# A decoder trunk on one core: two more raw weight tiles per group in spare result tiles, the sum t4 made last, the activations transposed two k-tiles later

## The chip, the cores and the metric

The kernel runs on one core of a Trainium2 chip. The metric is the device time of one execution in microseconds (us), the median of several. The core's engines run side by side, each through its own queue of instructions in order: TensorE (PE: matmuls, and PEld for its weight loads), VectorE (DVE), ScalarE (ACT), GpSimd (POOL) and SyncE (SP), which here only issues the DMA transfers from HBM.

## What is computed

256 tokens of width 2048 pass through two layers in float32. Layer 0 mixes by retention, layer 1 by latent attention, and each mixer is followed by a SwiGLU feed-forward of width 5632. The parts that matter here:

```
h = rms_norm(x, norm_mix_pre)
q, k, v, g = split(h @ ret_w_in)              # retention: 8 heads, k 256, v 512
y = retention(rope(q), rope(k), v); h = (silu(g) * groupnorm(y)) @ ret_w_out
x = x + rms_norm(h, norm_mix_post)
h = rms_norm(x, norm_ffn_pre)
gate, up = split(h @ w_gu); x = x + rms_norm((silu(gate) * up) @ w_down, norm_ffn_post)
```

## The kernel before, in words

**Products.** A float32 product is made of three matmuls in a narrower form (fp32r): every operand x is split into hi (x rounded, a cast on ACT, L204) and lo (x minus hi, a subtraction on DVE, L205), and hi·hi, hi·lo and lo·hi are added up in one PSUM bank. The weights arrive as raw tiles of 128 x 1024 float32 (512 KB), are split on the chip, and are the moving operand, 512 columns in one matmul.

**Groups.** A large product is cut into groups. A group multiplies all 256 tokens (two tiles t = 0, 1 of 128) by 1024 columns (two halves c = 0, 1 of 512) over 16 k-tiles, and keeps four PSUM banks (t, c). There are 4 groups for q and k (`qk_group`), 8 for v and g (`vg_group`, one per head) and 11 for gate and up in each layer (`swiglu`). The first group of q/k and of gate/up runs plainly (`group`, L263). All the others run through `first_sevens` (L415).

**first_sevens.** Its first n pairs of k-tiles (n = 4 in gate/up, 3 in v/g, 2 in q/k) are multiplied by a scheme with seven products instead of eight (Strassen's, in Winograd's form), which needs sums of the four blocks b00, b01, b10, b11 of a pair of raw tiles. It comes in stages:

1. `begin(p)`, for each pair p: loads the two raw tiles (L440 into the tag "raw", L443 into "y4"), makes t1 = b00 + b01 (L448), t2 = t1 + b11 (L449) and t3 = b01 + b11 (L452), and splits b00 and t2 (tile b) and t1, t3 (tile a). Nine matmuls of pair p and three of pair p-1 follow. After the last pair, the four banks are combined: m1 is copied out (L471, ACT), u is added up (L475, DVE), v is added in its bank and copied (L478 DVE, L479 ACT), and the banks of c01 (L482) and c11 (L485) are set, both on DVE.
2. `rest(p)`, for each p: splits the second raw tile whole (tile c). Three matmuls per pair go to bank (0,0), then three per pair to bank (0,1), which holds c01.
3. `fourth(p)`, for each p: t4 = t2 + b10 (L463, DVE, in place in t2), split into half a tile d. Three matmuls per pair go to bank (1,0), which must have been copied by L479.
4. The remaining k-tiles (8 in gate/up, kt 8 to 15) run plainly: load, split whole, 12 matmuls each.

**Slots.** Tiles come from tagged pools with a fixed number of slots. "raw" has RAW = 4, the split tiles "whi" and "wlo" have WB = 5 each and "mv" has MV = 6: t2 of every pair, m1 and u lie in "mv". The results of a stage wait in their own tags until its second product: "yT" (8 slots, retention) and "aT" (11 slots, feed-forward). What is not yet filled of these is lent out: `spare` gives the last one or two k-tiles (kt 14 and 15) their hi and lo tiles there. For q/k a tag "spare" of two slots does the same.

**What sets the order.** The source emits a plan; `step()` counts k-tiles, and `later(k, fn)` puts work behind k further ones. The final order on each engine is worked out when the program is built: an instruction whose operands or whose slot are not there yet by that reckoning lets later ones pass. The slots of one tag go out in the order of the source. So DVE, ACT and SP run ahead into the next group while PE works, until slots stop them.

**After a group** of gate/up, ACT makes silu(gate) (L993), DVE the product a (L995, tile "fa"), and `transposes(j, t, a)` (L957) turns it on PE into PSUM (L962, tile "ftp"), from where ACT copies it to aT (L963). `later(2 + t, ...)` on L998 puts these into `begin(1)` of the next group, behind the nine matmuls of pair 0.

**After a group** of v/g, `mixed` (L873) makes the head's output z, which is transposed (L902, "ztp") and copied into yT (L906) at `later(10, ...)`.

Of the kernel before, what the change touches and what calls it, by code (L numbers as in the profile page):

```python
# [8 lines left out]
F32 = mybir.dt.float32  # L9
F32R = mybir.dt.float32r  # L10
# [5 lines left out]
P = 128  # L16
# [41 lines left out]
def trunk(  # L58
# [73 lines left out]
    def later(k, fn):  # L132
        order[0] += 1
        todo.append((steps[0] + k, order[0], fn))
# [63 lines left out]
    wp = ctx.enter_context(tc.tile_pool(name="wp", bufs=1))  # L198
    RAW, WB, MV = 4, 5, 6

    def split(hi, lo, src, g=None):

        if g is None:
            nc.scalar.copy(out=hi, in_=src)  # L204
            nc.vector.tensor_sub(out=lo, in0=src, in1=hi.bitcast(F32))  # L205
        else:
            nc.scalar.activation(out=hi, in_=src, func=AF.Copy, scale=g)
            nc.vector.scalar_tensor_tensor(
                out=lo, in0=src, scalar=g, in1=hi.bitcast(F32), op0=ALU.mult, op1=ALU.subtract
            )  # L210

    def weights(load, parts, name, room=None):

        raw = wp.tile([P, 1024], F32, tag="raw", bufs=RAW, name=f"{name}_raw")
        load(raw)
        if room is None:
            hi = wp.tile([P, 1024], F32R, tag="whi", bufs=WB, name=f"{name}_hi")
            lo = wp.tile([P, 1024], F32R, tag="wlo", bufs=WB, name=f"{name}_lo")
        else:
            hi, lo = room(f"{name}_xhi"), room(f"{name}_xlo")  # L220
        for a, n, g in parts:
            split(hi[:, a : a + n], lo[:, a : a + n], raw[:, a : a + n], g)
        return hi, lo, raw
# [191 lines left out]
    def first_sevens(lhs, kts, w, g, name, n, left, spare):  # L415
# [44 lines left out]
        def fourth(p):  # L460
            if p % 2 == 0:
                last[0] = parts("d")
            nc.vector.tensor_add(out=t2[p], in0=t2[p], in1=raw1[p][:, 0:512])  # L463
            wt["d", p] = half(last[0], p % 2)
            split(*wt["d", p], t2[p])

        kept = {}

# [61 lines left out]
        carry_out(plan, banks, cols, {})  # L530
        return banks

    def tile_load(w, g, name, halves=0, spare=(0, None)):

        def load(kt, first_half=False):
            n = 512 if kt < halves or first_half else 1024

            def dma(raw):
                for a in range(0, 1024, 512 if kt < halves else 1024):
                    m = 512 if kt < halves else 1024
                    nc.sync.dma_start(out=raw[:, a : a + m], in_=w[g, kt, :, a : a + m])

            parts = [(a, n, None) for a in range(0, 512 if first_half else 1024, n)]
            return weights(dma, parts, f"{name}_w{kt}", spare[1] if kt >= DT - spare[0] else None)

        return load

# [186 lines left out]
    def retention():  # L737
# [40 lines left out]
        def vg_group(h, spare):  # L778
            return first_sevens(h_lhs, DT, ret_vg, h, f"rvg{h}", VG_SEVENS, lambda p: ins[p], spare)

        with tc.tile_pool(name="rt_s", bufs=1) as sp:
# [63 lines left out]
            with tc.tile_pool(name="rt_q", bufs=1) as rp:  # L845
                rope_c = rp.tile([P, NT, NF_R], F32, name="rope_c")
                rope_s = rp.tile([P, NT, NF_R], F32, name="rope_s")
                spare = 1, lambda name: rp.tile([P, 1024], F32R, tag="spare", bufs=2, name=name)
                for gq in range(4):
                    banks = qk_group(gq, spare)  # L850
                    if gq == 0:
                        rx = [rms(first[t], D, "rx", f"first_r{t}") for t in range(NT)]
                        rotary_tables()
                        for t in range(NT):
                            for dst, src in ((rope_c, cos_t), (rope_s, sin_t)):
                                nc.vector.tensor_scalar(
                                    dst[:, t, :], src[:, t, 0:NF_R], scalar1=rx[t], scalar2=None,
                                    op0=ALU.mult,
                                )
                    head_scores(gq, rotated(banks, rope_c, rope_s, rp), rp)  # L860
                banks = vg_group(0, spare)

            with tc.tile_pool(name="rt_v", bufs=1) as rp:

                yT = {}

                def spare_y(name):
                    return rp.tile([P, 1024], F32R, tag="yT", bufs=RH, name=name)

                def take_y(k0, n):  # L870
                    return yT[k0 // 4][:, k0 % 4 : k0 % 4 + n]
# [40 lines left out]

                for h in range(RH):
                    if h:
                        banks = vg_group(h, (min(2, (RH - h) // 2), spare_y))
                    vh = rp.tile([P, NT, RV], F32R, tag="vh", bufs=1, name=f"vh{h}")
                    vl = rp.tile([P, NT, RV], F32R, tag="vl", bufs=1, name=f"vl{h}")
                    ph = rp.tile([P, 3 * P], F32R, tag="ph", bufs=1, name=f"ph{h}")
                    pl = rp.tile([P, 3 * P], F32R, tag="pl", bufs=1, name=f"pl{h}")
                    split(ph, pl, scores[h])  # L920
                    sg = rp.tile([P, NT, RV], F32, tag="sg", bufs=1, name=f"sg{h}")
                    for t in range(NT):
                        split(vh[:, t, :], vl[:, t, :], banks[t][0], rx[t])
                        nc.scalar.activation(
                            out=sg[:, t, :], in_=banks[t][1], func=AF.Silu, scale=rx[t]
                        )
                    for t in range(NT):
                        later(2 + t, lambda h=h, t=t, pr=(ph, pl), v=(vh, vl), sg=sg: mixed(h, t, pr, v, sg))
# [16 lines left out]
    def swiglu(i):  # L945
        with tc.tile_pool(name=f"ff{i}", bufs=1) as fp:

            groups = FF // 512
            aT = {}

            def spare_a(name):
                return fp.tile([P, 1024], F32R, tag="aT", bufs=groups, name=name)

            def take_a(k0, n):
                return aT[k0 // 4][:, k0 % 4 : k0 % 4 + n]

            def transposes(j, t, a):  # L957
                if t == 0:
                    aT[j] = fp.tile([P, 4, NT, P], F32, tag="aT", bufs=groups, name=f"aT{i}{j}")
                tp = misc_bank(f"ftp{i}{j}{t}")  # L960
                for b in range(4):
                    nc.tensor.transpose(tp[:, b * P : (b + 1) * P], a[:, b * P : (b + 1) * P], ident)  # L962
                nc.scalar.copy(  # L963
                    out=aT[j][:, :, t, :], in_=tp.rearrange("p (j q) -> p j q", j=4)
                )

            def sums(n=0):
                f = wp.tile([P, 4, P], F32, tag="mv", bufs=MV, name=f"sf{i}")
                if n < 2:
                    hi = fp.tile([P, 4, P], F32R, tag="sa", bufs=4, name=f"sh{i}")  # L970
                    lo = fp.tile([P, 4, P], F32R, tag="sa", bufs=4, name=f"sl{i}")
                else:
                    hi = wp.tile([P, 4, P], F32R, tag="ah", bufs=3, name=f"sh{i}")
                    lo = wp.tile([P, 4, P], F32R, tag="al", bufs=3, name=f"sl{i}")
                return f, hi, lo

            ins, where = gu_next[0]
            where[0] = sums

            for j in range(groups):  # L980
                name = f"gu{i}_{j}"
                spare = min(2, (groups - j) // 2), spare_a
                if j:
                    banks = first_sevens(
                        h_lhs, DT, w_gu[i], j, name, GU_SEVENS, lambda p: ins[p], spare
                    )
                else:
                    banks = group(h_lhs, DT, tile_load(w_gu[i], j, name, 0, spare), name, lead=4)
                watch[0] = None
                both = fp.tile([P, NT, 512], F32, tag="fa", bufs=1, name="fa")  # L990
                for t in range(NT):
                    sg = fp.tile([P, 512], F32, tag="fsg", bufs=2, name="fsg")
                    nc.scalar.activation(out=sg, in_=banks[t][0], func=AF.Silu, scale=rx_next[t])  # L993
                    a = both[:, t, :]
                    nc.vector.scalar_tensor_tensor(  # L995
                        out=a, in0=banks[t][1], scalar=rx_next[t], in1=sg, op0=ALU.mult, op1=ALU.mult
                    )
                    later(2 + t, lambda j=j, t=t, a=a: transposes(j, t, a))  # L998
            closing(
                take_a, FF // P, w_down[i], g_ffn_post[i],  # L1000
                None if i else G_MIX + DT, f"dn{i}",
                lambda name: fp.tile([P, 1024], F32, tag="fa", bufs=1, name=name), sevens=DN_SEVENS, sums=sums,
            )
# [373 lines left out]
```

## Time and profile before

| | |
|---|---|
| median of 3 runs | 2427.42 us (2424.3 to 2428.29) |
| the profiled execution's own time | 2426.71 us |
| its span, first to last instruction | 2424.9 us |
| busy share of the span | PE 99%, PEld 81%, DVE 88%, ACT 61%, POOL 1% |
| mean granted TensorE clock | 0.998 of full speed |
| matmuls | 10888 |

A matmul of 512 columns is shown with 390 ns, but the next one starts about 227 ns after it: they overlap, so that PE looks busy even in short waits. A wait of PE is therefore read from the distance between starts, or from the idle time of PEld and PE that the views name. Rows of a timeline have: start, duration, engine, line, operation, out<-in, shape, count, and in brackets the idle time before and what ended it. DVE's additions are shown with 0.68 us (512 columns) and 1.21 us (1024), but follow each other at 0.60 and 1.14 us.

### The profile page before, as it was taken

To read this page: it belongs to the slowest core of one execution; us is meant where nothing else is said; L and a number is where in the kernel's file an instruction comes from. 1 tells how busy PE (TensorE), PEld (TensorE's weight loads), DVE (VectorE), ACT (ScalarE), POOL (GpSimd) and SP (SyncE) were. 2 spreads that over 40 slices of the span, in tenths; PEclk is the share of its full clock that TensorE was granted. 3 is DMA by queue.
4 is the path that set the end of the run, shared out by engine and by line. 5 is a ranking of instruction groups with operands and counts; after the bars stand their busy time and mean duration, and the time that the engine had idled before them with its cause. 6 is when DMAs were issued, how large, how long until landed. Compare 5 with 4: busy or idle time off the path is not lost.

```text
span 2424.9 us, 30707 instructions
## 1 busy us (share of the span) xinstructions
PE 2403.3 (99%) x10888; PEld 1975.1 (81%) x10888; DVE 2122.0 (88%) x3034; ACT 1479.1 (61%) x2082; POOL 23.9 (1%) x38
## 2 busy tenths in 40 slices
PE   9999999999999999999999999999999999999998
PEld 7888888888888787888888888888877888888887
DVE  8878989887879999899989987876899999998997
ACT  6545666665656666666666665655666666666664
POOL 0000000000000000000000000000000000000000
PEclk9999999999999999999999999999999999999999
DMA  7565565556665565656456654446656565556655
GB/s 273 171 211 185 164 206 194 165 172 203 192 213 193 195 213 184 217 172 216 168 194 214 207 185 148 130 137 198 202 182 215 180 211 202 188 183 202 206 194 164
DMA packets 129610, 463.75 MB, mean 191 GB/s; under 512 B 14640, under 2 KB 15024, under 8 KB 129456
## 3 DMA queue, kind: packets, MB, share of 16 engines
q1 hardware_dynamic: 129456, 461.80, 57.7%
q8 instruction: 85, 1.39, 0.2%
q14 instruction: 69, 0.57, 0.1%
HBM read 459.64 MB, written 2.10 MB: 190 GB/s over the span
## 4 chain that ended last, share of the span: by engine, by line
PE 80%; DVE 12%; DMA 4%; issue 2%; ACT 2%; SPq 0%; POOL 0%; DVEq 0%; ACTq 0%; POOLq 0%
PE gu_b L409 23%; PE dn_b L409 16%; PE rvg_b L409 14%; PE rto_b L409 6%; PE rqk_b L409 5%; PE mlo_b L409 3%; PE q L409 3%; PE dn_m L409 3%; DMA gu_w_raw<-w_gu 2%; DVE gu_blo L205 2%; DVE gu_alo L205 1%; PE mc_b L409 1%; DVE gu_w_lo L205 1%; DVE gu_t L449 1%; DVE gu_clo L205 1%
## 5 line engine op out<-in xcount | busy, mean ns | idle before, releaser
L409 PE MATMUL gu_b<-gu_w_hi,hT 128*128 128x512 f32 x1248 | 342.0, 390 | 0.0
L409 PEld LDWEIGHTS gu_b<-gu_w_hi,hT 128*128 128x128 f32 x1248 | 233.1, 188 | 49.0 <-DVE hT L205 0.9
L204 ACT CAST dn_w_hi<-dn_w_raw 128x1024 fp32r<-128x1024 f32 (+1 forms) x176 | 172.8, 993 | 95.2 <-DMA dn_w_raw<-w_down 44.4
L205 DVE TENSOR_TENSOR gu_w_lo<-gu_w_raw,gu_w_hi 128x1024 fp32r<-128x1024 f32 x156 | 185.5, 1218 | 48.4 <-ACT gu_w_hi L204 48.3
L204 ACT CAST gu_w_hi<-gu_w_raw 128x1024 fp32r<-128x1024 f32 x156 | 158.1, 1048 | 92.9 <-DMA gu_w_raw<-w_gu 73.2
L205 DVE TENSOR_TENSOR dn_w_lo<-dn_w_raw,dn_w_hi 128x1024 fp32r<-128x1024 f32 (+1 forms) x176 | 196.1, 1146 | 9.2 <-ACT dn_w_hi L204 8.9
L409 PE MATMUL gu_b<-gu_w_lo,hT 128*128 128x512 f32 x624 | 193.3, 390 | 0.0
L409 PE MATMUL dn_b<-dn_w_hi,dn_ah 128*128 128x512 f32 x536 | 169.3, 390 | 0.0
L409 PE MATMUL dn_b<-dn_w_lo,dn_ah 128*128 128x512 f32 x536 | 169.0, 389 | 0.0
L409 PE MATMUL dn_b<-dn_w_hi,dn_al 128*128 128x512 f32 x536 | 168.9, 389 | 0.0
L409 PE MATMUL rvg_b<-rvg_w_hi,hT 128*128 128x512 f32 x552 | 149.8, 390 | 0.0
L409 PEld LDWEIGHTS gu_b<-gu_w_lo,hT 128*128 128x128 f32 x624 | 116.6, 188 | 25.3 <-DVE gu_w_lo L205 1.3
L409 PEld LDWEIGHTS rvg_b<-rvg_w_hi,hT 128*128 128x128 f32 x552 | 103.4, 188 | 21.4
L409 PEld LDWEIGHTS dn_b<-dn_w_hi,dn_al 128*128 128x128 f32 x536 | 100.6, 188 | 21.0
L409 PEld LDWEIGHTS dn_b<-dn_w_lo,dn_ah 128*128 128x128 f32 x536 | 100.6, 188 | 20.9
L409 PEld LDWEIGHTS dn_b<-dn_w_hi,dn_ah 128*128 128x128 f32 x536 | 100.3, 188 | 20.4
L409 PE MATMUL rqk_b<-rqk_w_hi,hT 128*128 128x512 f32 x384 | 106.0, 392 | 2.2 <-ACT rqk_w_hi L204 1.5
L204 ACT CAST gu_ahi<-gu_ta 128x1024 fp32r<-128x1024 f32 x80 | 84.3, 1054 | 35.1 <-DVE gu_ta L452 17.1
L205 DVE TENSOR_TENSOR rvg_w_lo<-rvg_w_raw,rvg_w_hi 128x1024 fp32r<-128x1024 f32 x69 | 82.3, 1222 | 25.5 <-ACT rvg_w_hi L204 25.1
L204 ACT CAST gu_bhi<-gu_t 128x512 fp32r<-128x512 f32 x80 | 49.7, 621 | 85.9 <-DVE gu_t L449 85.8
L204 ACT CAST rvg_w_hi<-rvg_w_raw 128x1024 fp32r<-128x1024 f32 x69 | 71.1, 1051 | 46.0 <-DMA rvg_w_raw<-ret_vg 34.7
L205 DVE TENSOR_TENSOR gu_alo<-gu_ta,gu_ahi 128x1024 fp32r<-128x1024 f32 x80 | 97.7, 1221 | 0.0
(487 smaller groups left out, 6109.5 us busy)
## 6 DMA issues: line engine op xcount, KB each, us to landing
gu_w_raw<-w_gu SPq DMA_DIRECT2D x192, 512.0 KB, 4.3
dn_w_raw<-w_down SPq DMA_DIRECT2D x176, 512.0 KB, 4.4
gu_s<-w_gu SPq DMA_DIRECT2D x160, 512.0 KB, 4.4
rvg_w_raw<-ret_vg SPq DMA_DIRECT2D x80, 512.0 KB, 4.4
rto_w_raw<-ret_out SPq DMA_DIRECT2D x64, 512.0 KB, 4.4
rqk_w_raw<-ret_qk SPq DMA_DIRECT2D x51, 512.0 KB, 4.5
rvg_s<-ret_vg SPq DMA_DIRECT2D x48, 512.0 KB, 4.3
mlo_w_raw<-mla_out SPq DMA_DIRECT2D x32, 512.0 KB, 3.6
```

The costliest lines, as they stand in the source:

```text
L204: nc.scalar.copy(out=hi, in_=src)
L205: nc.vector.tensor_sub(out=lo, in0=src, in1=hi.bitcast(F32))
L409: nc.tensor.matmul(out, e[2](), e[3](), start=bank not in begun, stop=ends[bank, added.get(bank, 0)] == n, skip_group_check=bank in added,)
L449: nc.vector.tensor_add(out=t2[p], in0=ta[:, 0:512], in1=b11)
```

## The change

It has three parts. First, `share` hands out the spare slots anew: two raw tiles (kt 12 and 13; one, kt 13, where slots are short) now go there too, so they no longer pass through the four "raw" slots; the hi and lo tiles of kt 14 and 15 keep their place where six slots or more are free, those of kt 15 alone where three to five are, none below. For q/k, the tag "spare" has three slots. Second, t4 gets a tile of its own in "mv" instead of being made in place. Third, the transposes of the activations come at `later(4 + t, ...)`, in `begin(2)` of the next group.

```
+    def share(slots, room):
+        both = 2 if slots >= 6 else 1 if slots >= 3 else 0
+        return min(2, slots - 2 * both), both, room
...
-    def weights(load, parts, name, room=None):
-        raw = wp.tile([P, 1024], F32, tag="raw", bufs=RAW, name=f"{name}_raw")
+    def weights(load, parts, name, raw_room=None, room=None):
+        if raw_room is None:
+            raw = wp.tile([P, 1024], F32, tag="raw", bufs=RAW, name=f"{name}_raw")
+        else:
+            raw = raw_room(F32, f"{name}_xraw")
...
-            nc.vector.tensor_add(out=t2[p], in0=t2[p], in1=raw1[p][:, 0:512])
+            t4 = wp.tile([P, 512], F32, tag="mv", bufs=MV, name=f"{name}_t4")
+            nc.vector.tensor_add(out=t4, in0=t2[p], in1=raw1[p][:, 0:512])
             wt["d", p] = half(last[0], p % 2)
-            split(*wt["d", p], t2[p])
+            split(*wt["d", p], t4)
...
-            return weights(dma, parts, f"{name}_w{kt}", spare[1] if kt >= DT - spare[0] else None)
+            raws, both, room = spare
+            return weights(
+                dma, parts, f"{name}_w{kt}", room if DT - 2 - raws <= kt < DT - 2 else None,
+                room if kt >= DT - both else None,
+            )
...
-                spare = 1, lambda name: rp.tile([P, 1024], F32R, tag="spare", bufs=2, name=name)
+                spare = share(3, lambda kind, name: rp.tile([P, 1024], kind, tag="spare", bufs=3, name=name))
...
-                        banks = vg_group(h, (min(2, (RH - h) // 2), spare_y))
+                        banks = vg_group(h, share(RH - h, spare_y))
...
-                spare = min(2, (groups - j) // 2), spare_a
+                spare = share(groups - j, spare_a)
...
-                    later(2 + t, lambda j=j, t=t, a=a: transposes(j, t, a))
+                    later(4 + t, lambda j=j, t=t, a=a: transposes(j, t, a))
```

## Rows read from the trace of the kernel before

**Rows 1.** The page: busy time of the engines, chain that ended last.

```profile
PE 2403.3 (99%) x10888; PEld 1975.1 (81%) x10888; DVE 2122.0 (88%) x3034; ACT 1479.1 (61%) x2082; POOL 23.9 (1%) x38
...
PE 80%; DVE 12%; DMA 4%; issue 2%; ACT 2%; SPq 0%; POOL 0%; DVEq 0%; ACTq 0%; POOLq 0%
```

**Rows 2.** Windows (length, then PE, PEld, DVE, ACT, POOL busy, clock, DMA): shortest group, both layers.

```profile
995.19:1037.04 41.85, 41.85 (x189) 34.51 (x188) 38.08 (x49) 26.34 (x34) 0.00 (x0) 1.00 0.62 201
780.84:1165.13 384.29, 380.71 (x1694) 310.03 (x1693) 356.49 (x455) 241.15 (x308) 0.00 (x0) 1.00 0.60 197
1759.57:2142.28 382.71, 381.01 (x1693) 309.89 (x1692) 356.76 (x456) 242.30 (x311) 0.00 (x0) 1.00 0.59 198
```

**Rows 3.** Waits of PEld, whole span: waiter, releaser, total us, times, longest.

```profile
PEld gu_b L409 <- ACT gu_mv L479: 5.8, 8, 0.9
PEld ftp L962 <- DVE fa L995: 5.3, 13, 0.8
PEld gu_b L409 <- DVE gu_b L482: 5.3, 12, 0.7
```

**Rows 4.** Timeline of DVE, last stages of gate/up group 8 in layer 0.

```profile
1125.97 0.68 DVE L463 TENSOR_TENSOR gu_t<-gu_t,gu_s 128x512 f32<-128x512 f32 x1
...
1131.98 2.35 DVE L205 TENSOR_TENSOR gu_clo<-gu_s,gu_chi 128x1024 fp32r<-128x1024 f32 x2
...
1138.91 2.48 DVE L205 TENSOR_TENSOR gu_dlo<-gu_t,gu_dhi 128x512 fp32r<-128x512 f32 x4
```

**Rows 5.** Windows: group 8's full DVE stretch, the stretch after it, v/g group 3.

```profile
1131.98:1142.53 10.55, 10.53 (x47) 8.35 (x46) 10.55 (x15) 9.04 (x13) 0.00 (x0) 1.00 0.67 212
...
1142.50:1153.90 11.40, 11.40 (x52) 9.45 (x51) 8.28 (x9) 5.71 (x6) 0.00 (x0) 1.00 0.82 273
...
338.94:353.07 14.13, 14.13 (x65) 11.50 (x65) 14.12 (x24) 10.56 (x17) 1.10 (x2) 1.00 0.37 110
```

**Rows 6.** Timeline of ACT, then of PE, gate/up group 8 in layer 0.

```profile
1130.37 1.05 ACT L204 CAST gu_chi<-gu_s 128x1024 fp32r<-128x1024 f32 x1 [0.36 <-PE gu_b L409]
...
1125.51 0.66 PE L962 MATMUL ftp<-cst,fa 128*128 128x128 f32 x4 [0.24 <-DVE fa L995]
...
1134.65 0.39 PE L409 MATMUL gu_b<-gu_ahi,sl 128*128 128x512 f32 x1
...
1143.82 0.61 PE L409 MATMUL gu_b<-gu_w_lo,hT 128*128 128x512 f32 x2
```

**Rows 7.** Timeline of PE, gate/up groups 3 and 2 in layer 0.

```profile
921.36 0.39 PE L409 MATMUL gu_b<-gu_ahi,sl 128*128 128x512 f32 x1
...
924.57 0.50 PE L409 MATMUL gu_b<-gu_dhi,hT 128*128 128x512 f32 x1 [0.31 <-ACT gu_mv L479]
...
931.05 0.61 PE L409 MATMUL gu_b<-gu_w_lo,hT 128*128 128x512 f32 x2
...
887.12 0.61 PE L409 MATMUL gu_b<-gu_w_hi,hT 128*128 128x512 f32 x2
887.67 0.50 PE L409 MATMUL gu_b<-gu_dhi,hT 128*128 128x512 f32 x1
```

**Rows 8.** Timelines of DVE, then of PE, v/g groups 3 and 4.

```profile
379.44 1.89 DVE L463 TENSOR_TENSOR rvg_t<-rvg_t,rvg_s 128x512 f32<-128x512 f32 x3
...
351.85 4.62 DVE L205 TENSOR_TENSOR rvg_w_lo<-rvg_w_raw,rvg_w_hi 128x1024 fp32r<-128x1024 f32 x4
...
348.07 0.60 PE L902 MATMUL ztp<-cst,z 128*128 128x128 f32 x4
...
353.69 0.62 PE L409 MATMUL rvg_b<-rvg_w_lo,hT 128*128 128x512 f32 x2
...
375.00 0.60 PE L902 MATMUL ztp<-cst,z 128*128 128x128 f32 x4
```

**Rows 9.** Timeline of SP, gate/up group 8 in layer 0.

```profile
1129.62 0.33 SPq L544 DMA_DIRECT2D gu_w_raw<-w_gu  x1
1133.22 5.53 SPq L443 DMA_DIRECT2D gu_s<-w_gu  x4
```

More of the change, by code (lines that the diff above doesn't have):

```diff
@@ L219, in weights @@
         else:
-            hi, lo = room(f"{name}_xhi"), room(f"{name}_xlo")
+            hi, lo = room(F32R, f"{name}_xhi"), room(F32R, f"{name}_xlo")
         for a, n, g in parts:
@@ L531, in first_sevens, with tile_load @@
         return banks
-    def tile_load(w, g, name, halves=0, spare=(0, None)):
+    def tile_load(w, g, name, halves=0, spare=(0, 0, None)):
         def load(kt, first_half=False):
@@ L865, in retention, with spare_y @@
                 yT = {}
-                def spare_y(name):
-                    return rp.tile([P, 1024], F32R, tag="yT", bufs=RH, name=name)
+                def spare_y(kind, name):
+                    return rp.tile([P, 1024], kind, tag="yT", bufs=RH, name=name)
                 def take_y(k0, n):
@@ L949, in swiglu, with spare_a @@
             aT = {}
-            def spare_a(name):
-                return fp.tile([P, 1024], F32R, tag="aT", bufs=groups, name=name)
+            def spare_a(kind, name):
+                return fp.tile([P, 1024], kind, tag="aT", bufs=groups, name=name)
             def take_a(k0, n):
```

## The prediction

> **What bounds the kernel now.** I read the page first: PE is busy 99% of the span and the chain that ended last runs on PE for 80% of it, on DVE for 12% [rows 1]. So the question is how much time PE still loses, and to whom. That is read from the windows, one for each gate/up group: the shortest takes 41.85 us [rows 2], which I take as PE's own pace. The two long windows hold nine group periods each, 384.29 and 382.71 us [rows 2], that is 767.0 / 18 = 42.61 us a group. The most that any part of this change can return in gate/up is therefore 0.76 us a group, 15.2 us over the 20 groups made by `first_sevens`. Next the waits of PEld [rows 3]: three releasers stand out, the bank copied by L479 (8 times), the activation product "fa" ahead of the transposes (13 times, 5.3 us, never more than 0.8) and the bank set by L482 (12 times). 8 + 12 = 20: in each group PE waits once for a bank, in the "early" groups for L479, in the "late" ones for L482. Last the timelines. In late group 8, DVE makes its four t4 early, the first at 1125.97, before the c parts begin at 1131.98 [rows 4], and is then busy 10.55 of 10.55 us [rows 5] with c parts, bank work, d parts and w_lo of kt 8: one closed queue on which PE's next operands hang.
>
> **The change part by part.** *Transposes later.* Today PE arrives at the transposes after nine matmuls and finds "fa" not made, as at 1125.51, where it stood idle 0.24 us [rows 6]. Two k-tiles later is 12 matmuls later, 2.7 us at 0.227 us each, more than the longest of those waits, 0.8 us [rows 3]. All 13 go. What is late next is nothing on PE: the matmuls that move ahead of the transposes are of pair 1, whose a and b parts DVE makes before. The four L963 copies on ACT come later with them, ahead of the casts of the last pairs; ACT is busy 26.34 of 41.85 us [rows 2] and takes that in. After the last group the transposes fall in the down-projection, at its k-tiles 4 and 5, where activations of groups long finished are multiplied; cost 0. PEld's 5.3 us overlap partly with running matmuls, so the gain lies between 0 and 5.3; I take 4.0, about 0.3 for each wait, nearer to the waits' sum because the 0.24 at 1125.51 is PE's own idle time: **-4.0 us**.
>
> *t4 last.* The addition costs the same, but it needs a slot of "mv" now. Four t2, m1 and u fill all six, and slots go out in the order of the source, so the first t4 of gate/up cannot be made before u or m1 is read for the last time, after L482 or L485. Four additions, 4 x 0.60 = 2.4 us, leave a stretch where DVE had time and enter the closed one. The queue behind them: ACT's dhi casts wait for t4, and the casts of kt 8 and after stand behind these; DVE's dlo waits for dhi; PE waits for dlo. Work it out on group 8. The closed stretch can't start earlier than the first chi cast, which ends at 1130.37 + 1.05 = 1131.42, and that cast waited for PE to free a slot [rows 6]. Its content was 10.5 us and becomes 12.9, so w_lo of kt 8 is done at 1144.4. PE asks for it at 1143.82, and had started its last a-matmul at 1134.65 [rows 6]: 9.17 us, in which 39 matmuls need 39 x 0.227 = 8.85. New lateness 0.58 us; PE can put one matmul more in the wait, 0.23, which leaves +0.33 a group, and 12 late groups give **+4.0**. The bounds of this term: -0.3 a group if PE finds other work for the whole wait, +0.6 if none. In early groups the d parts are made so early that PE takes a d-matmul first and waits with it for L479's bank, as at 924.57; from the last a-matmul, 921.36, to w_lo of kt 8, 931.05, it needs 9.69 us [rows 7]. With t4 late they become groups of the late kind, 1144.4 - 1134.65 = 9.75 less the extra matmul, 9.5: -0.17, 8 times, **-1.4** (bounds: -0.8 a group if the whole wait goes, down to 39 matmuls; +0.1 at 9.75).
>
> In v/g three t4 go the same way: 1.8 us, today at the boundary of groups (379.44 [rows 8]), enter the stretch 338.94 to 353.07, in which DVE is busy 14.12 of 14.13 [rows 5]. There u, m1 and three t2 leave one slot, so the first t4 follows u and the others follow the banks. w_lo of kt 6, the first in its row, was done at 351.85 + 1.22 = 353.07, PE asks for it at 353.69 [rows 8]: 0.6 of the 1.8 is covered, 1.2 is not. Two hi matmuls (0.45) and the four transposes "ztp" (0.6 as shown) may fill it: between 0 and +1.2 a group, and as one of the two fillers is likely used otherwise I take 0.6; 8 groups: **+4.8** (0 to 9.6). In q/k two additions in three groups: no row is nearer than v/g's, whose 0.6 of cover takes half of 1.2; I take 0.17 a group, **+0.5** (0 to 1.8).
>
> *Raw tiles in spare slots.* kt 12 and 13 can be loaded before the "raw" slots come round. After the closed stretch DVE is busy 8.28 of 11.40 us, the 3.1 us being waits for raw tiles, but PE in the same window is busy 11.40 of 11.40 [rows 5]. So the time that DVE gains is idle time that costs nothing: **0**. The Trainium skill (Perfetto Trace Analysis, Optimization Strategy) reads a repeating gap as a sign of too few buffers for the next tile, which would speak for this part; by it 3.1 us of DVE in each of 20 groups, 62 us, would be at stake, and this trace gives PE none of it. SP issues the two loads in its gap between the load at 1129.62 and the next pair's at 1133.22, 0.33 us each [rows 9], so nothing is queued behind them; POOL is untouched. Where slots are short (gate/up groups 6, 7 and 9, heads 3, 4 and 6) the hi and lo of kt 14, or of 15, return to the ring of WB = 5 that all earlier k-tiles use; that DVE idle time hides it: 0, at most 2 us in all, both ways.
>
> *The sum.* -4.0 + 4.0 - 1.4 + 4.8 + 0.5 = +3.9 on the profiled execution's own 2426.7 us: **2430.6 us**. That execution lies 0.7 below the median of the runs, 2427.4. About 0.2% (4.9 us) is what a measurement of this kernel can tell from no change, so 2430.6 counts as the same.
>
> **The rivals.** *Faster: PE steps around the late d parts.* When the program's order on PE is worked out anew with t4 late, matmuls of kt 8 may be put ahead of those of d, as 887.12 stands ahead of 887.67 [rows 7]. Then the bank waits of all groups go too and gate/up groups near 41.95 us: (42.61 - 41.95) x 20 = 13.2 less, v/g costing +2.4: 2426.7 - 13.2 + 2.4 = **2416**. For it: the shortest group [rows 2] shows that the pace can be had, and that waits of this kind came in each group [rows 3]. Against it: it needs w of kt 8 early, and DVE makes w_lo behind the d parts at 1138.91 [rows 4].
>
> *Slower: t4 stands in the closed stretch without cover.* The full 2.4 us reach PE where its slack ends: gate/up late +0.6 x 12 = 7.2, v/g +1.2 x 8 = 9.6, q/k +0.5, transposes -4.0: +13.3, **2440**. It decides as soon as DVE's stretch from the first chi to w_lo exceeds about 12.3 us (1143.82 - 1131.42 = 12.4) and PE finds no other matmul. For it: DVE is without a gap there [rows 5]. PE also stood still at 924.57 [rows 7] though other matmuls were behind it. Beside it stands a sentence of the Trainium skill (TensorE: Matmul & The Clock Gate, Part 2: What happens when you issue a matmul): matmuls keep program order, only weight loads are pulled ahead; by that rule, a late d part holds all that follows and the whole lateness counts, and the wait at 924.57 agrees.
>
> *Slower: a raw tile behind yT.* In v/g, kt 13's slot comes after the slot of the head before. That head's transposes run as filler at 348.07, where the load has time; should the new order put them at a place like 375.00 [rows 8], its k-tile would wait some 2.6 us in 7 groups: +18 on the forecast, **2448**.
>
> *The change doesn't do what it says:* where "mv" is not full (v/g, q/k), t4 may stay early by the order worked out. Then these 5.3 us fall away, 2425; that lies within the forecast's own range.
>
> **How the numbers follow.** Forecast (little change, own range 2423 to 2436): 0.38. Faster rival, 2416: 0.30. Slower rival without cover, 2440: 0.27. The yT rival: 0.05. The range 2414 to 2442 leaves out a third of the faster case (0.10), a fifth of the slower one (0.05) and the yT case (0.05). It is set by the unknown cost in the closed stretch: -0.3 to +0.6 in gate/up, 0 to 1.2 in v/g. Faster: 0.30. Same: the forecast without its top end, 0.34. Slower: 0.27 + 0.05 + 0.04 = 0.36. The clock is not in question: it was granted at 1.00, its upper level of 2.4 GHz, in all the windows [rows 2, 5].
>
> **What the changed profile would show.** Transposes right: no waits of PEld on "ftp" for "fa". t4 right: the t4 rows of DVE behind L482 and L485, the stretch from clo to w_lo without a gap and some 2.4 us longer; the waits on L482 or new ones on dlo and w_lo near 0.6 us show the slower rival, group periods near 42.0 the faster one. Raw tiles right: DVE's gap of 3.1 us gone and PE's row in that window unchanged. I am wrong in kind if group periods fall below 42.2 us (the bank waits went too), if v/g groups change by more than 1.2 us, or if a wait on a load stands on PE's chain.

## The result and the profile after

The changed kernel takes 2439.3 us (median of 5 runs, 2437.12 to 2440.61) against 2427.42: a ratio of 1.005, 95% interval 1.0035 to 1.0064. It is slower by half a per cent. The forecast was 2430.6, counted as no change. The time lies inside the stated range, 0.7 us from the price of the slower rival, 2440. The runs below show that this closeness is mostly luck: two terms were wrong by some 13 and some 20 us, in opposite directions.

The page of the changed kernel, in the order of [rows 1]: busy time of the engines, then the chain that ended last.

```profile
PE 2406.5 (99%) x10888; PEld 1973.3 (81%) x10888; DVE 2121.0 (87%) x3034; ACT 1471.6 (60%) x2082; POOL 25.0 (1%) x38
...
PE 80%; DVE 12%; issue 3%; ACT 2%; DMA 2%; SPq 0%; POOL 0%; DVEq 0%; POOLq 0%; ACTq 0%
```

Nothing can be read from it: the shares are those of before. Lines after `share` have moved by 5 to 15, so L205 is now L210, L463 is L473, L482 is L492. The waits of PEld say more; they answer to [rows 3].

```profile
PEld gu_b L418 <- DVE gu_dlo L210: 16.0, 20, 0.9
PEld rvg_b L418 <- DVE rvg_dlo L210: 7.1, 10, 1.0
PEld gu_b L418 <- DVE gu_w_lo L210: 5.3, 22, 0.3
...
PEld gu_b L418 <- DVE gu_b L492: 2.7, 6, 0.7
```

All three waits of before have shrunk or gone: none of "ftp" on "fa", none worth naming on the bank copied by ACT, 6 in place of 12 on the bank set by DVE. A new one is there in every one of the 20 groups: PE waits for dlo, the low part of t4. The windows, as in [rows 2]: one group, then the nine periods of layer 0, nine of layer 1, and seven periods of v/g.

```profile
961.62:1004.25 42.63, 42.25 (x190) 34.44 (x188) 40.34 (x53) 27.42 (x37) 0.00 (x0) 1.00 0.58 198
788.91:1176.51 387.60, 382.30 (x1694) 309.33 (x1692) 355.81 (x454) 239.24 (x308) 0.00 (x0) 1.00 0.58 196
1769.23:2154.51 385.28, 381.38 (x1693) 309.58 (x1692) 354.27 (x452) 239.46 (x308) 0.00 (x0) 1.00 0.58 197
200.18:521.51 321.33, 317.38 (x1416) 258.34 (x1415) 277.93 (x383) 190.65 (x273) 6.59 (x12) 1.00 0.53 180
```

Gate/up grew from 767.0 to 772.9 us, v/g from 315.74 to 321.33. The span grew by 12.8 us (2424.9 to 2437.7), and 11.5 of these stand here. What has changed is the shape: fourteen of the eighteen gate/up periods are now within 0.05 us of 42.63, where before they scattered from 41.85 to 43.51. One wait of one size has taken the place of several.

That wait in the group that starts at 961.62: first DVE, then ACT, then PE.

```profile
969.97 2.54 DVE L210 TENSOR_TENSOR gu_clo<-gu_s,gu_chi 128x1024 fp32r<-128x1024 f32 x2 [0.31 <-ACT gu_chi L209]
...
977.09 1.89 DVE L473 TENSOR_TENSOR gu_t<-gu_t,gu_s 128x512 f32<-128x512 f32 x3
978.90 1.89 DVE L210 TENSOR_TENSOR gu_dlo<-gu_t,gu_dhi 128x512 fp32r<-128x512 f32 x3
...
977.86 1.82 ACT L209 CAST gu_dhi<-gu_t 128x512 fp32r<-128x512 f32 x3 [2.33 <-DVE gu_t L473]
...
978.87 0.39 PE L418 MATMUL gu_b<-gu_dhi,hT 128*128 128x512 f32 x1
979.63 0.50 PE L418 MATMUL gu_b<-gu_dlo,hT 128*128 128x512 f32 x1 [0.38 <-DVE gu_dlo L210]
979.97 0.62 PE L418 MATMUL gu_b<-gu_dhi,hT 128*128 128x512 f32 x2
...
982.27 0.39 PE L418 MATMUL gu_b<-gu_dhi,hT 128*128 128x512 f32 x1
982.58 0.74 PE L418 MATMUL gu_b<-gu_w_lo,hT 128*128 128x512 f32 x2
```

The sums t4 stand behind the c parts, as forecast, three of them ahead of the first dlo. ACT stands idle 2.33 us until the first t4 is made, and PE's step from 978.87 to 979.63 is 0.76 us in place of 0.23. That is +0.53 for dlo; the next step, 0.34, is another +0.11, and w_lo of kt 8 (982.27 to 982.58) +0.08, with another +0.11 behind it: 0.83 us in all. The Trainium skill (TensorE: Matmul & The Clock Gate, Part 2: What happens when you issue a matmul) says that matmuls keep program order and only weight loads move ahead; the trace agrees, since the matmuls at 979.97, on a dhi that PE had used at 978.87 already, stood behind the waiting one.

### The profile page after: what moved, and what is told of

The parts are those of the page before. It is cut to its first block, busy times and chain, and to the rows that moved or that the text cites. A ratio compares the mean times of both kernels' runs of the same rounds, so it can differ in the third digit from the quotient of the medians.

```text
span 2437.7 us, 30763 instructions
## 1 busy us (share of the span) xinstructions
PE 2406.5 (99%) x10888; PEld 1973.3 (81%) x10888; DVE 2121.0 (87%) x3034; ACT 1471.6 (60%) x2082; POOL 25.0 (1%) x38
## 4 chain that ended last, share of the span: by engine, by line
PE 80%; DVE 12%; issue 3%; ACT 2%; DMA 2%; SPq 0%; POOL 0%; DVEq 0%; POOLq 0%; ACTq 0%
PE gu_b L418 25%; PE dn_b L418 16%; PE rvg_b L418 12%; PE rto_b L418 6%; PE rqk_b L418 6%; PE mlo_b L418 4%; PE q L418 3%; PE dn_m L418 3%; DVE gu_clo L210 2%; DVE gu_t L473 1%; PE mc_b L418 1%; ACT gu_chi L209 1%; PE rto_m L418 1%; DMA gu_w_raw<-w_gu 1%; DMA gu_s<-w_gu 1%
## 5 line engine op out<-in xcount | busy, mean ns | idle before, releaser
L418 PE MATMUL gu_b<-gu_w_hi,hT 128*128 128x512 f32 x1296 | 357.5, 391 | 0.0
L418 PEld LDWEIGHTS gu_b<-gu_w_hi,hT 128*128 128x128 f32 x1296 | 242.1, 188 | 51.3 <-DVE hT L210 0.8
L210 DVE TENSOR_TENSOR dn_w_lo<-dn_w_raw,dn_w_hi 128x1024 fp32r<-128x1024 f32 (+1 forms) x176 | 196.4, 1147 | 13.1 <-ACT dn_w_hi L209 12.7
L418 PE MATMUL gu_b<-gu_w_lo,hT 128*128 128x512 f32 x648 | 202.7, 393 | 0.0
L210 DVE TENSOR_TENSOR gu_w_lo<-gu_w_raw,gu_w_hi 128x1024 fp32r<-128x1024 f32 x122 | 145.0, 1217 | 13.6 <-ACT gu_w_hi L209 13.6
L418 PE MATMUL rvg_b<-rvg_w_hi,hT 128*128 128x512 f32 x576 | 155.4, 389 | 0.0
L209 ACT CAST gu_w_hi<-gu_w_raw 128x1024 fp32r<-128x1024 f32 x122 | 123.8, 1047 | 38.8 <-DMA gu_w_raw<-w_gu 27.6
L210 DVE TENSOR_TENSOR gu_clo<-gu_s,gu_chi 128x1024 fp32r<-128x1024 f32 x80 | 97.1, 1220 | 16.7 <-ACT gu_chi L209 15.5
L210 DVE TENSOR_TENSOR gu_alo<-gu_ta,gu_ahi 128x1024 fp32r<-128x1024 f32 x80 | 97.8, 1222 | 5.6 <-ACT gu_ahi L209 5.4
L209 ACT CAST rto_w_hi<-rto_w_raw 128x1024 fp32r<-128x1024 f32 (+1 forms) x64 | 64.2, 1011 | 45.6 <-PE rto_b L418 19.9
```

The source lines that it names most:

```text
L418: nc.tensor.matmul(out, e[2](), e[3](), start=bank not in begun, stop=ends[bank, added.get(bank, 0)] == n, skip_group_check=bank in added,)
```

## The experiments

Theory A, formed from these rows: the late t4 is the whole loss. Rival B: it is the late release of the second raw tiles, which t4 reads. (The first run's text gives the letter B to another rival, described there.) Rival C: the spare slots cost something too, because in the changed kernel the first and the ninth gate/up periods are long (44.75 and 44.35 us in layer 0).

Each ratio below is against the kernel before, timed beside the run; its medians were 2425.39, 2426.41 and 2426.95 us in the three rounds of runs, and 2427.42 beside the changed kernel. A difference between times of different rounds is therefore good to some 2 us only.

### The three parts by themselves

**Transposes alone.**

```diff
-                    later(2 + t, lambda j=j, t=t, a=a: transposes(j, t, a))
+                    later(4 + t, lambda j=j, t=t, a=a: transposes(j, t, a))
```

> The kernel before with the transposes of the activations two k-tiles later and nothing else. Theory A (the late t4 alone makes the change slower, because its additions enter DVE's full stretch): the waits on fa go (5.3 us of PEld) and nothing takes their place, 2421 to 2424 us. Rival B (PE is held later in each group anyway, by the banks of L479 and L482, so that an earlier start only makes that wait longer): 2426 to 2428, with the bank waits grown by what the fa waits lost.

2424.58 us, ratio 0.9997 (0.9988 to 1.0006): no change, where theory A had a gain. The waits on fa are gone, and others have taken their place. That is what rival B of this run said, though most of the growth is on clo, which it did not name:

```profile
PEld gu_b L409 <- DVE gu_b L482: 6.5, 12, 0.7
PEld gu_b L409 <- DVE gu_clo L205: 5.8, 13, 1.0
PEld gu_b L409 <- ACT gu_mv L479: 5.3, 7, 0.8
```

The wait on clo rose from 2.7 us before to 5.8, that on L482 from 5.3 to 6.5, while L479 stayed near its 5.8. PE came sooner to operands that DVE made no sooner.

**Raw tiles alone**, that is the changed kernel with t4 in place and the transposes at `2 + t`:

```diff
-            t4 = wp.tile([P, 512], F32, tag="mv", bufs=MV, name=f"{name}_t4")
-            nc.vector.tensor_add(out=t4, in0=t2[p], in1=raw1[p][:, 0:512])
+            nc.vector.tensor_add(out=t2[p], in0=t2[p], in1=raw1[p][:, 0:512])
...
-                    later(4 + t, lambda j=j, t=t, a=a: transposes(j, t, a))
+                    later(2 + t, lambda j=j, t=t, a=a: transposes(j, t, a))
```

> The kernel before with the new sharing of the spare slots and nothing else. Theory A: the loads move, PE does not see it, 2426 to 2428.5 us. Rival C (the spare slots themselves cost: loads of the next group come bunched, and the ring of five gets kt 14 back in the late groups): 2431 us or more, with the periods of the first and the ninth of the gate/up groups some 1.5 us longer, as in the changed kernel.

2412.12 us, ratio 0.9944 (0.9931 to 0.9956). Neither theory had a gain. The windows of the two layers:

```profile
779.50:1157.87 378.37, 377.11 (x1693) 310.91 (x1692) 356.61 (x455) 240.69 (x308) 0.00 (x0) 1.00 0.60 200
1751.56:2128.81 377.25, 376.85 (x1694) 310.96 (x1692) 356.30 (x454) 241.39 (x308) 0.00 (x0) 1.00 0.61 201
```

755.6 us in place of 767.0: most gate/up groups now run at 41.7 to 41.8 us, which the prediction had called PE's own pace. How can a gap of DVE that lies beside a busy PE be worth that? The rows of DVE at the start of the next group show it. The group is the one that [rows 4] call group 8 (counted from 0 among the ten of `first_sevens`, so j = 9), with the last of kt 8 to 15, the first sum t1, and the first c part. Before, PE starts it at 1122.62:

```profile
1109.10 1.22 DVE L205 TENSOR_TENSOR gu_w_lo<-gu_w_raw,gu_w_hi 128x1024 fp32r<-128x1024 f32 x1 [1.00 <-ACT gu_w_hi L204]
...
1111.46 0.69 DVE L448 TENSOR_TENSOR gu_ta<-gu_s 128x512 f32<-128x512 f32 x1
...
1130.84 1.22 DVE L205 TENSOR_TENSOR gu_alo<-gu_ta,gu_ahi 128x1024 fp32r<-128x1024 f32 x1
```

With the raw tiles alone, PE starts the same group at 1116.16:

```profile
1103.41 0.69 DVE L457 TENSOR_TENSOR gu_ta<-gu_s 128x512 f32<-128x512 f32 x1
...
1123.30 1.22 DVE L210 TENSOR_TENSOR gu_alo<-gu_ta,gu_ahi 128x1024 fp32r<-128x1024 f32 x1
1124.53 2.53 DVE L210 TENSOR_TENSOR gu_clo<-gu_s,gu_chi 128x1024 fp32r<-128x1024 f32 x2
```

DVE's lead, from its first sum to PE's first matmul of the group, was 1122.62 - 1111.46 = 11.2 us and is 1116.16 - 1103.41 = 12.8 (the group ahead of this one, j = 8, lends only one raw tile). Before, DVE was still at the last a part when chi was ready at 1131.42, and began with clo at 1131.98, 9.36 us into the group [rows 4, 6]; now it begins at 8.37. All that follows, up to the banks of L479 and L482, moves with it. The table gives the medians over the 20 groups, worked out in the same way:

| kernel | lead of DVE's first sum | clo begins after PE's start |
|---|---|---|
| before | 11.2 us | 9.1 us |
| one raw tile in spare slots (below) | 12.8 us | 8.5 us |
| raw tiles alone | 14.4 us | 8.4 us |
| raw tiles and transposes | 14.6 us | 8.4 us |
| changed kernel | 11.2 us | 8.4 us |

8.4 is where the first chi comes ready: from there on a longer lead returns nothing more.

That a group goes by its first c part can be read in the kernel before by itself. In ten of its eighteen periods all four t4 stand ahead of the c parts. There the first c part begins 8.67 to 9.95 us after PE's start, and the period less that time is between 33.1 and 33.2 us in every one. The two ends are neighbours: the group from 995.19 takes 41.85 us [rows 2], the next, from 1037.04, takes 43.09, and their first c parts are these:

```profile
1003.86 2.36 DVE L205 TENSOR_TENSOR gu_clo<-gu_s,gu_chi 128x1024 fp32r<-128x1024 f32 x2
...
1046.99 1.22 DVE L205 TENSOR_TENSOR gu_clo<-gu_s,gu_chi 128x1024 fp32r<-128x1024 f32 x1
```

The transposes alone changed each of these ten periods by what they changed in the start of its first c part, to within 0.04 us: the waits on fa had stood ahead of that point, and so their end returned nothing.

The other eight periods are the first four of each layer. There three, three, two and one of the four t4 stood behind the first c part already in the kernel before, and the period less its start is 33.8 to 34.1 us. With the raw tiles alone only the first group of each layer keeps one such t4, and the difference is 33.3 to 33.5 everywhere. Of the 11.4 us that gate/up gains, the ten periods have 4.6 (their first c parts came 6.7 us earlier in sum, but not all of that counts) and six of the eight have 6.5, with first c parts only 2.8 us earlier. So a part of the gain is that these t4 moved ahead again; no run measures that part by itself.

**Transposes and raw tiles**, t4 in place as above.

> The changed kernel with t4 made in place again. Theory A: 2421 to 2424 us, the same as with the transposes alone, no wait on d parts. Rival C: 2428 us or more, with the long first and ninth gate/up groups still there.

2409.82 us, ratio 0.9938 (0.9925 to 0.995): better than A expected, and the fastest version found. It beats the kernel before by 15.6 us and the changed kernel by 29.5 (by the two ratios, some 27). One group and the two layers:

```profile
948.83:990.55 41.72, 41.72 (x190) 34.59 (x188) 39.82 (x52) 26.65 (x35) 0.00 (x0) 1.00 0.58 202
780.95:1157.51 376.56, 376.20 (x1693) 311.20 (x1692) 356.39 (x454) 238.90 (x307) 0.00 (x0) 1.00 0.60 201
1749.48:2125.68 376.20, 376.20 (x1693) 311.23 (x1692) 355.65 (x453) 240.01 (x308) 0.00 (x0) 1.00 0.60 202
```

PE is busy in the whole of layer 1's window. With raw tiles in place the transposes are worth about 2.3 us more (2412.12 to 2409.82); the intervals of the two ratios overlap, so that this last step is small rather than measured.

**t4 alone**, the first hunk of the change on t4 in the kernel before.

> The kernel before with t4 in a tile of its own and nothing else. Theory A: the whole loss and no gain from the transposes: waits of PEld on dlo of some 16 us in gate/up and 7 in v/g, 2440 to 2446 us. Rival C: less than half of the loss, 2427 to 2433 us.

2455.95 us, ratio 1.0124 (1.0109 to 1.014): more than A expected. By spans the parts add up: t4 costs 2453.5 - 2424.9 = 28.6 us on the kernel before and 2437.7 - 2408.0 = 29.7 on the other two parts. Rival C falls: the spare slots are the gain of the change, not a cost.

### Which property of the late t4 costs

**t4 early, copied late.** The slots of the second raw tiles come free as before, and four late instructions stay.

```diff
+            nc.vector.tensor_add(out=t2[p], in0=t2[p], in1=raw1[p][:, 0:512])
             t4 = wp.tile([P, 512], F32, tag="mv", bufs=MV, name=f"{name}_t4")
-            nc.vector.tensor_add(out=t4, in0=t2[p], in1=raw1[p][:, 0:512])
+            nc.vector.tensor_tensor(out=t4, in0=t2[p], in1=t2[p], op=ALU.max)
```

> The changed kernel, but the sum t4 is made in place and early, so that the second raw tile's slot comes free as before, and a plain copy of it (max of t4 with itself, also 512 columns) goes into the late tile. Theory A (the four late instructions of DVE stand in front of the first d part, whose cover was 1.3 us): the loss stays, 2436 to 2443 us, waits on dlo near 16 us in gate/up. Rival B (the late t4 holds the slots of the second raw tiles, so that the loads of the next group come late): most of the 29 us between the third run and the changed kernel goes, 2411 to 2420 us.

2443.32 us, ratio 1.0075 (1.0058 to 1.0092). The loss stays, at 42.6 us a group, with the same 16.0 us of waits on dlo: rival B falls as the cause of the loss. What it names is real but small. DVE's lead is 13.0 us here, 11.2 in the changed kernel, and the ninth periods of the two layers take 42.76 and 42.63 us in place of 44.35 and 43.71.

**t4 made twice**, by a second copy of the addition's line.

> The changed kernel with the addition t4 made twice, one after the other. Theory A: three more additions of 0.60 us stand in front of the first d part of each gate/up group, with no cover left, +1.8 us in 20 groups, and 1.2 to 1.8 us in each v/g group: 2480 to 2495 us. Rival B: the slots of the second raw tiles are held 0.6 us longer each, which is a small step: 2439 to 2447 us.

2511.66 us, ratio 1.0358 (1.0343 to 1.0374). The direction is A's, the size is beyond it. A gate/up group takes 45.15 us in place of 42.63, +2.5: all four additional instructions count in full (4 x 0.60 = 2.4), not only the three that A had ahead of the first d part.

**First t4 in a slot of its own, v/g and q/k in place.**

```diff
-            t4 = wp.tile([P, 512], F32, tag="mv", bufs=MV, name=f"{name}_t4")
+            if n == 4 and p:
+                t4 = wp.tile([P, 512], F32, tag="mv", bufs=MV, name=f"{name}_t4")
+            elif n == 4:
+                t4 = own[0].tile([P, 512], F32, tag="t4", bufs=1, name=f"{name}_t4")
+            else:
+                t4 = t2[p]
```

> The changed kernel, but in gate/up the first t4 of a group has a slot of its own, outside mv, so that it can be made early and frees the slot of t2 for the next; in v/g and q/k t4 is made in place. Theory A: a separate tile costs nothing, only the place in DVE's queue does: 2408 to 2413 us, as with the transposes and the raw tiles alone, and the rows of t4 stand before the c parts again. If the tile as such costs: 2420 us or more.

2424.15 us, ratio 0.999 (0.9981 to 1.0): the expectation failed, because the edit did not do what was meant. DVE's rows of the group that starts at 951.05:

```profile
951.76 0.68 DVE L479 TENSOR_TENSOR gu_t<-gu_t,gu_s 128x512 f32<-128x512 f32 x1
...
966.52 0.68 DVE L211 TENSOR_TENSOR gu_dlo<-gu_t,gu_dhi 128x512 fp32r<-128x512 f32 x1
967.12 1.89 DVE L479 TENSOR_TENSOR gu_t<-gu_t,gu_s 128x512 f32<-128x512 f32 x3
968.92 1.29 DVE L211 TENSOR_TENSOR gu_dlo<-gu_t,gu_dhi 128x512 fp32r<-128x512 f32 x2
```

Only the first t4 is early. The other three come behind u in the order of the slots of "mv", although t2's slot is free by then, and stand before the second dlo. So the run became a dose: 0 late additions give 41.75 us a group, three 42.36, four 42.63, four doubled 45.15. The separate tile, which the first t4 has here too, has no price that shows; the place in DVE's queue has.

**Late t4 in v/g and q/k only** (`n < 4`, in place for gate/up).

> The changed kernel with t4 made in place in gate/up and in its own late tile in v/g and q/k. Theory A: 0.9 us for each of 8 v/g groups, up to 1 us back in q/k: 2415 to 2419 us, so that some 20 of the 29 us belong to gate/up. If the loss comes from anything that both share (the slots mv between groups): 2425 us or more.

2417.84 us, ratio 0.9968 (0.9956 to 0.9979), as expected: 8.0 us above the version without late t4. The other 21.5 us to the changed kernel are gate/up's.

### What the raw tiles give

Theory D: a raw tile in a spare slot gives DVE lead, and lead is worth something until the first c part no longer waits for DVE.

**One raw tile in place of two**, on "raw tiles alone":

```diff
-        return min(2, slots - 2 * both), both, room
+        return min(1, slots - 2 * both), both, room
```

> The kernel before with the new sharing, but with one raw tile (kt 13) in the spare slots in place of two. Theory D (a raw tile in a spare slot lets DVE begin the next group's sums earlier, which the banks then show): between the kernel before and the second run, 2414 to 2421 us, DVE's first sum of a group near 12.8 us ahead of PE's first matmul of it, between 11.2 and 14.4. Rival E (the gain is that of the order alone, worked out anew, and does not go by the number of tiles): at either end, 2410 to 2413 or 2424 to 2428 us.

2412.98 us, ratio 0.9939 (0.9922 to 0.9955). The lead came out as expected (12.8 us), the time did not: one tile returns what two return, since clo already begins at 8.5 us. Rival E's "either end" fits the time, but the lead went by the number of tiles, which E denies; the gain saturates.

**Three slots for raw tiles in the kernel before**, `RAW, WB, MV = 3, 5, 6`.

> The kernel before with three slots for raw tiles in place of four. Theory D: the first sum of a group starts 1.5 to 3 us later on DVE, and with no lead left all of that is on PE's path: 30 gate/up and v/g groups or so by 1 to 3 us, 2445 to 2510 us. Rival (raw loads are hidden anyway, as the prediction had it): 2426 to 2432 us.

2546.08 us, ratio 1.049 (1.0474 to 1.0505): beyond the upper end. The lead fell to 6.5 us, clo begins 12.8 us into the group, and gate/up groups take about 46 us. The loads are not hidden, they were at the edge. The run mixes two effects, though: in every group three or four of the four t4 also fell behind the first c part.

**Additional early work**, one instruction ahead of each split of t4, on the kernel before:

```diff
             nc.vector.tensor_add(out=t2[p], in0=t2[p], in1=raw1[p][:, 0:512])
+            nc.vector.tensor_tensor(out=t2[p], in0=t2[p], in1=t2[p], op=ALU.max)
```

> The kernel before with one more instruction of 0.60 us on DVE for each early t4 (max of t2 with itself), 2.4 us in a gate/up group, 1.8 in a v/g group. Theory D: DVE has no lead there, so gate/up groups get 1 to 2.4 us longer: 2445 to 2475 us. Rival (the early stage has slack on DVE, as the prediction took it): 2426 to 2431 us.

2487.16 us, ratio 1.0245 (1.023 to 1.026): beyond the upper end. A gate/up group grew by (405.82 - 384.29) / 9 = 2.4 us, just what was added, but not by the path that D names. The first c part begins 9.8 us into a group, only 0.7 later than before. In eighteen of the twenty groups two of the four additions and three of the four new instructions slipped behind it (more in the other two), so that the last t4 ends 19 us into a group and the last d part 24.0 in place of 18.8. So this run shows again that the stretch of the c and d parts has no room, and says little about the lead. The window of layer 0:

```profile
790.37:1196.19 405.82, 392.04 (x1693) 307.38 (x1692) 378.17 (x490) 240.19 (x308) 0.00 (x0) 1.00 0.56 187
```

**The same additional early work** on transposes and raw tiles, by the same edit:

> The same additional early instructions on the third run (transposes and raw tiles, t4 in place). Theory D: DVE's lead of 3.2 us there takes in the 2.4 us: 2409 to 2415 us, gate/up groups still at 41.75 us. Rival (any work of DVE ahead of the c parts costs): 2420 us or more.

The window of layer 0:

```profile
783.74:1165.11 381.37, 379.04 (x1694) 310.04 (x1692) 376.02 (x492) 238.95 (x308) 0.00 (x0) 1.00 0.60 199
```

2427.63 us, ratio 1.0002 (0.9993 to 1.0011), 17.8 us above the version without it (15.5 by the spans): D's forecast failed, the time is in the rival's range. A group takes (381.37 - 376.56) / 9 = 0.53 us more, where the kernel before paid 2.4. In gate/up four fifths of the added work cost nothing, not all of it as expected: up to three of the four new instructions are ordered behind the first c part here too, and the last d part ends 20.6 us into a group (median) in place of 18.0. The twenty groups make up some 10 of the 15.5 us; the rest lies outside them and its cause is open.

## Why the prediction was right and wrong

**Transposes, -4.0: right in mechanism, wrong in what comes next.** The waits on fa went, as said. "What is late next is nothing on PE" failed: next was DVE, and alone the part returned nothing (0.9997). Only with DVE ahead does some of it appear, about 2.3 us, which is small beside the noise.

**Raw tiles, 0: wrong, the one part whose effect was missed altogether.** Measured: -13.3 us. The step that failed is "the time that DVE gains is idle time that costs nothing", inferred from PE being busy 11.40 of 11.40 us in that window [rows 5]. The idle time does not hurt where it stands; it is carried into the next group, where DVE begins its sums 3 us later than it could and has used up all of its lead when the first c part is due. The row was there: chi ended at 1131.42, clo began at 1131.98 [rows 4, 6]. The prediction took the chi cast, and so PE, as the gate of the stretch, and passed over the 0.56 us in which DVE itself was late. The Trainium skill (Perfetto Trace Analysis, Optimization Strategy) says that a gap repeating on the engine that should be saturated can mean too little room for the next tile. The prediction weighed this and set it aside. Here the gap stood on DVE, beside a busy PE, and it did mean too few buffers. Of the 62 us that the prediction put at stake, some 13 came.

**t4, +7.9 in all: right in place and direction, too small.** Measured: +29.5 us, by the ratios some 27. The move into DVE's closed stretch, the slots of "mv" as the reason, the order dhi, dlo, PE: all shown. The size failed at "PE asks for it at 1143.82": the cover was taken at w_lo of kt 8, behind the d parts, but the first dlo is due earlier and has its own cover. In the version without late t4, dlo of the group at 948.83 begins on DVE at 964.29, and PE uses it at 966.29:

```profile
964.29 2.49 DVE L210 TENSOR_TENSOR gu_dlo<-gu_t,gu_dhi 128x512 fp32r<-128x512 f32 x4
...
966.29 0.39 PE L418 MATMUL gu_b<-gu_dlo,hT 128*128 128x512 f32 x1
```

The first of the four, 0.68 us long, ends near 964.97, so the cover is 1.3 us; three additions of 0.60 are 1.8, and 0.5 remains, which is PE's +0.53 above. With the steps behind it 0.88 us a group, where the forecast had +0.33 in twelve and -0.17 in eight. (The forecast's own 0.58 less 0.23 is 0.35 rather than 0.33, 0.2 us over twelve groups.) For the "early groups" the premise failed as well: not all of their d parts were made early. Three, three, two and one of their t4 stood behind the first c part before the change, and their last d part ended 18.8 to 22.3 us into the group, that of the late groups 18.1 to 19.4. Their bank wait did end, but that was the raw tiles' doing. In v/g 0.9 us a group (6.4 us more over seven periods than without late t4, 321.33 against 314.92), inside its bounds of 0 and 1.2.

**The lead, which no term had.** In the changed kernel the raw tiles' gain in lead, 3.2 us, is used up again (11.2 in the table). In part w_lo of kt 8 is late, and with it the raw slots; in part the late t4 hold the slots of the second raw tiles, since with these free early, and w_lo as late, the lead is 13.0. DVE still starts the c parts in time, as t4 no longer stands before them. Where a group lends one raw tile less, in front of the ninth period, the lead is 9.2 us and that group takes 44.35 us in place of 42.63. The lead does not explain the long first period (11.6 us there); its cause stays open.

**The rivals.** The slower rival named the right wait, and its 2440 is 0.7 us from the result, but its terms were +16.8 for gate/up and v/g (7.2 + 9.6) with -4.0 for the transposes, where the runs have some +28 for t4 and about -16 for the transposes and the raw tiles together. The faster rival's reason (PE steps around the late d parts) was not seen: PE waited for dlo in all 20 groups. Yet its level for the groups, near 41.95 us, is what the change without t4 reaches. Neither the yT rival nor the one that the change does not do what it says was seen: v/g periods are the same with the raw tiles alone (44.7 to 44.9 us against 44.7 to 45.1), and t4 moved late in v/g and in two of the three q/k groups.

**The tests named.** No wait on fa, t4 rows behind the bank work, waits of up to 0.9 us on dlo: as listed for the slower rival. "DVE's gap of 3.1 us gone" was not seen: DVE's idle time in a gate/up group is 3.3 us (median), and was 3.0 before, counted in the same way. In layer 0's nine periods DVE's waits for hi of the raw tiles were 27.1 us before and are 20.3; its waits for chi, of which there were none, are 7.0.

## What to carry to other kernels

Idle time of an engine that feeds the bound one is not free because the bound engine is busy at that moment: follow it to the next point where the two meet, and measure the lead that is left there. When work is moved into a full queue, take the cover at the first operand behind it, not at the last. And when a change has several parts, run each alone: here one part's loss of nearly 30 us hid a gain of 16.

## What was not expected of the hardware

A wait of PE costs more than the idle time that is shown for it. After 0.38 us of idle time PE's starts stood 0.76 us apart, 0.53 more than without a wait: the idle time is counted from the end of a matmul shown with 0.39 us, and so leaves out the 0.16 us by which two matmuls otherwise overlap (0.39 less 0.23). The step behind it was 0.34 in place of 0.23 us, and so it was after the wait at 924.57 [rows 7], where the next start is at 924.91. In the gate/up products of the kernel before and the changed kernel, all 50 steps between starts that were longer than 0.40 us were followed by one of 0.33 or 0.34. So each of these stalls had about 0.11 us of its own on top.
